# The r projection of an RWKV-7 layer, moved from the dense part into the pairs' projection jobs of the scan

## The chip, the core and the metric

The kernel runs on one core of a Trainium2 chip. The time is the device time of one execution in microseconds (us), from launch to end. The engines are TensorE (PE, whose weight loads are listed as PEld), VectorE (DVE), ScalarE (ACT), GpSimd (POOL) and SyncE (SP), which here only issues DMA transfers. Each engine works through its own queue in order and waits on semaphores for the others. TensorE's clock has two levels, 2.4 GHz and 1.2 GHz; the profile gives the granted share, 1.0 or 0.5, and its mean over a stretch.

## What is computed

One step of a two-layer network over 640 tokens (512 of a sample, 128 of a prompt) with 1024 features. Each layer is a SwiGLU feed-forward, a token mixer and a second feed-forward. Layer 0's mixer is a bidirectional RWKV-7, and only this is touched:

```python
xx = 0.5 * (hp[:, :-2] + hp[:, 2:]) - h
xs = h[None] + xx[None] * mu[:, None, None, :]
xr, xw, xk, xv, xa, xg = xs[0], xs[1], xs[2], xs[3], xs[4], xs[5]
rkv = jnp.einsum('nbtd,nde->nbte', jnp.stack([xr, xk, xv]), w_rkv)
...
def step(S, inp):
    r_t, w_t, k_t, v_t, kk_t, a_t = inp
    sa = jnp.einsum('bhij,bhj->bhi', S, -kk_t)
    S = (S * w_t[:, :, None, :]
         + sa[..., None] * (kk_t * a_t)[:, :, None, :]
         + v_t[..., None] * k_t[:, :, None, :])
    return S, jnp.einsum('bhij,bhj->bhi', S, r_t)
```

Six token streams are mixed from h and its neighbours. Three of them (r, k, v) go through 1024 x 1024 projections; the others through low-rank maps that give decays, rates and a gate. The recurrence then runs over the tokens in both directions, for 16 heads of 64.

## The kernel before

Features lie on the partitions, eight tiles of 128, and a tile of output features is a pair of heads, so there are eight pairs, 0 to 7. Tokens are cut into a first half of 384 and a second of 256 (in the dense part the cut is at 382, so that a token's neighbours are in the same part).

**The dense part** (`dense`) follows the first feed-forward. For each half and for each stream in `ORDER`, `stream` builds eight tiles on VectorE (line 466), stores them to DRAM if they are needed later (`keep`, line 470, streams 2 and 3 for k and v), and `project` multiplies them on TensorE in full float32 (line 502). Only pair 0's k and v are made here (`VD = 1`). Then come pair 0's key norm (lines 552 to 563), the gate's second map for all pairs (line 570) and, last, r for all eight pairs (lines 574 to 589): stream 0 is built and cut into a high and a low float32r part, each pair's weights as well (`wsplit`), and `mm3` makes three float32r products for one (lines 299 to 301), over 382 and 260 columns. The result goes through ACT (line 588) to DRAM, row `rkv[0][m]`.

**The scan** (`scan`) works on the pairs in overlapping periods. Pair m's `chain`, which carries the states from chunk to chunk, takes period m; its `products` and `solve` stand in period m - 1, its `prep` (loads of r, k, v, key transposes at line 744, decays) in period m - 2, and its `proj` (k and v, for pairs 1 to 7) in period m - 3. Each stage is a generator. `scan` gives each step a due time, spread evenly over the stage's window (`WIN`), and issues whichever is due first; the order in which instructions then stand on the engines is fixed when the program is built, by a scheduler that may move independent work a little. The periods have no fixed length: the chip runs the queues as they stand.

**A projection job** (`proj`) does its products in float32 over 320 columns: for j = 1, 2 (k, v) and each half of the tokens, eight products accumulate in bank `px`, with weights in `pw` tiles and the stream's tiles reloaded from DRAM into a ring of four (`mid`). A step ends after two products. The result is copied by ACT (`po`) and stored. Each such product shows as two records in the trace.

Other names: `c` products of the chain are lines 938, 949, 957 (bank `pc`), its outputs lines 975 to 981 (`po`), the products inside chunks line 810 (`pg`) and the transposed keys 819 (`pa`), the solve's recurrence lines 880 and 882 on VectorE, and its end, blocks of 32 x 32 products, lines 904, 905, 911 and 912 (`pm`). From the fifth period on, 60 products that nobody reads (`filler`, line 638) fill in for the projections.

Of the kernel before, what the change touches and what calls it, by code (L numbers as in the profile page):

```python
# [14 lines left out]
ALU = mybir.AluOpType  # L15
# [25 lines left out]
class Net:  # L41
# [15 lines left out]
    def psum(self, tag="ps"):  # L57
        """the next of a tag's banks"""
        if isinstance(tag, int):
            return self.ps.tile([P, 512], F32, tag=f"b{tag}", name=self.name("ps"))  # L60
        q = self.banks[tag]
        q.append(q.pop(0))
        return self.ps.tile([P, 512], F32, tag=f"b{q[-1]}", name=self.name(tag))
# [29 lines left out]
    def silu_cond(self):  # L93
        """2 silu(cond), on every partition"""
# [10 lines left out]
    def mods(self, layer, idx, ks=range(KD)):  # L105
        """modulation vector idx of a layer -> [P, KD, 2]"""
# [11 lines left out]
    def mods_first(self):  # L118
        """the first two modulation vectors, on the tensor engine"""
# [35 lines left out]
    def premod_scale(self, layer, sub, scale):  # L155
        """norm_pre * (1 + scale) -> [P, KD, 2]"""
# [13 lines left out]
    # -- 1/sqrt(mean + eps) of every token, from sums over each partition's features --  # L170
    def rstd(self, ss, n, eps, bank=None):
        """bank: a PSUM bank whose contents are no longer needed"""
# [28 lines left out]
    def part(self, hf, k, lo, dt=F32R):  # L201
        """one of the two parts of tile k of a product's moving operand"""
        return self.fp.tile([P, PARTW[hf]], dt, tag=f"h{'hl'[lo]}{hf}_{k}", name=self.name("hp"))

    def sumsq(self, srcs, hf):
        """sum over the tiles of squares, per partition"""
# [15 lines left out]
    def postnorm_gen(self, fps, hf, gp, eps, bank=None):  # L222
        """x += gp * f * rstd(f), f in PSUM; stops after the first half of the tiles"""
# [25 lines left out]
    def prenorm_gen(self, hf, gs, sh, dest, bank=None, r=None):  # L249
        """h = x * rstd(x) * gs + sh, every piece to the place that dest(tile, half) names"""  # L250
# [34 lines left out]
    def wsplit(self, src, eng=None):  # L285
        """a [P, up to 1024] block of weights as its two parts"""
# [16 lines left out]
    def ffn_s1(self, fi, hs, lead=0, early=()):  # L303
        """hs: per half a function that gives (hi, lo) tiles; returns g tiles"""
# [60 lines left out]
    def s2_step(self, hf, banks, outs, wh, wl, gh, gl, zero, first, last):  # L365
        """zero: zeros to open the banks with that two outputs share"""
# [15 lines left out]
ORDER = (1, 2, 4, 3, 5)  # L382
# [3 lines left out]
WQ = 256  # L386
FILL = (60, 4.8, 7.3)
# [3 lines left out]
class Rwkv:  # L391
# [31 lines left out]
    # Tokens 0..381 are one part of every stream, the rest the other: 382..511, two that mean nothing, the prompt.  # L423
    def dense_open(self, dram):
# [3 lines left out]
        self.xs = {j: dram.tile([P, KD, NT], F32, tag=f"xs{j}", name=f"xs{j}") for j in (1, 2)}  # L428
# [16 lines left out]
    def cut(self, hf, t, o=0):  # L445
        """the values of a part, o to the right"""
# [27 lines left out]
    def split_stream(self, i, hf):  # L474
        """a stream's part, every tile in two parts"""
        n, nc = self.n, self.nc
        out = []
        for k in range(KD):
            v, h, l = (self.view(hf, x) for x in (n.tmp(hf, WIDE[hf]), n.part(hf, k, 0), n.part(hf, k, 1)))
            nc.vector.scalar_tensor_tensor(v, self.xx[hf][k], self.vec[:, i, k:k + 1], self.cut(hf, self.h[hf][k], 1),  # L480
                                           op0=ALU.mult, op1=ALU.add)
            nc.scalar.activation(h, v, AF.Copy)
            (nc.vector if k % 3 == 1 else nc.gpsimd).tensor_tensor(l, v, h, op=ALU.subtract)  # L483
            out.append((h, l))
        return out

# [9 lines left out]
    def project(self, ws, xs, hf):  # L496
        """-> per block of weights [(first token, last, values in PSUM)]"""
# [11 lines left out]
    def dense(self, first):  # L509
        """first: the decay stream's part of the first tokens"""  # L510
# [29 lines left out]
        wr = {j: [self.load_w(t["w_rkv"][j, m]) for m in range(VD)] for j in (1, 2)}  # L540
        for hf in range(2):
            for i in ORDER:
                j = {2: 1, 3: 2}.get(i)
# [30 lines left out]
        xs = [self.split_stream(0, hf) for hf in range(2)]  # L574
        for m in range(KD):
            wh, wl = n.wsplit(t["w_rkv"][0, m])
            p = [self.view(hf, n.psum()) for hf in range(2)]
# [892 lines left out]
```

## Time and profile before

| | us |
|---|---|
| time, median of 3 runs | 3125.17 (3123.72 to 3130.29) |
| span of the profiled execution | 3110.3 |
| first feed-forward, up to the streams | about 0 to 541 |
| dense part without r | about 541 to 614 |
| r for all pairs | 614 to 677 |
| scan, periods -2 to 7 | 677 to about 1500 |
| rest of layer 0, and layer 1 | 1500 to 3110 |

The profiled execution's span runs from its first to its last instruction; it is a single execution, and its time stands beside the runs' as 3110.3 beside 3125.17. The periods' bounds are read from the times at which one pair's px products end and the next pair's begin: 677, 724, 780 (period 0), 884, 978, 1075, 1166, 1262 (period 5). In the tables of stretches, a busy time is the union of an engine's instructions; for TensorE it includes the last product's way through the array. The busy time of TensorE over the whole span is 2907.5 us (93%), of VectorE 1864.6 (60%), of ACT 1082.9 (35%) and of POOL 581.7 (19%).

### The profile page before, as it was taken

Reading aid. Unit: us, or ns where it says so; the run is one execution under the profiler, and the core shown is the slowest. Engines: PE = TensorE matmul, PEld = TensorE weight load, DVE = VectorE, ACT = ScalarE, POOL = GpSimd, SP = SyncE. Lnnn points to the kernel's source line nnn. Section 1 sums busy time; section 2 is a strip of 40 time slices with the busy share of each in tenths; the row PEclk is TensorE's granted clock in tenths of the full one; section 3 lists DMA queues with packets and bytes.
Section 4 is the critical chain, followed back from the end, with each engine's and each line's share of the span. In section 5 each row is a group of like instructions: output and inputs, shape, how many; then the busy total and the mean of one; then the engine's idle time right before and its main releaser. Section 6 shows DMA issues by size and latency. Waiting matters only on the chain.

```text
span 3110.3 us, 52692 instructions
## 1 busy us (share of the span) xinstructions
PE 2907.5 (93%) x21118; PEld 2588.4 (83%) x21118; DVE 1864.6 (60%) x3695; ACT 1082.9 (35%) x1892; POOL 581.7 (19%) x601
## 2 busy tenths in 40 slices
PE   8999998799999999999879999999999986999998
PEld 5999998585666666666779999999999986999997
DVE  7996338915647766566679995573333478432336
ACT  3122234423434444444341222452222455321233
POOL 2000033212212221121320002420001443000034
PEclk8999999997778888878889999999999997999999
DMA  6664235424323332012416664332212432222233
GB/s 242 215 215 165 89 122 187 152 97 148 96 79 106 120 104 90 30 48 78 165 56 208 224 224 160 128 106 95 82 68 102 140 120 85 82 75 76 89 122 123
DMA packets 163734, 382.05 MB, mean 123 GB/s; under 512 B 22432, under 2 KB 84512, under 8 KB 163232
## 3 DMA queue, kind: packets, MB, share of 16 engines
q1 hardware_dynamic: 161472, 375.60, 35.9%
q8 instruction: 166, 2.72, 0.4%
q10 hardware_dynamic: 2016, 3.07, 0.3%
q14 instruction: 80, 0.66, 0.1%
HBM read 352.19 MB, written 26.41 MB: 122 GB/s over the span
## 4 chain that ended last, share of the span: by engine, by line
PE 49%; DVE 7%; ACT 3%; issue 1%; DMA 0%; POOL 0%; SPq 0%; DVEq 0%; ACTq 0%; POOLq 0%
PE ps L300 14%; PE ps L299 14%; PE ps L301 14%; PE px L638 1%; DVE t L215 1%; DVE t L239 1%; ACT t L266 1%; PE pg L810 1%; DVE wl L294 1%; DVE t L242 0%; PE pa L737 0%; PE pc L949 0%; DVE x L243 0%; DVE sx L882 0%; ACT hp L275 0%
## 5 line engine op out<-in xcount | busy, mean ns | idle before, releaser
L299 PE MATMUL ps<-hp,wh 128*128 128x384 f32 (+2 forms) x3008 | 932.8, 312 | 14.7 <-ACT hp L275 10.4
L300 PE MATMUL ps<-hp,wh 128*128 128x384 f32 (+2 forms) x3008 | 934.4, 311 | 4.9 <-DVE hp L483 2.0
L301 PE MATMUL ps<-hp,wl 128*128 128x384 f32 (+2 forms) x3008 | 930.1, 310 | 2.9 <-DVE wl L294 2.9
L294 DVE TENSOR_TENSOR wl<-raw,wh 128x1024 fp32r<-128x1024 f32 x353 | 439.4, 1250 | 470.3 <-ACT wh L293 469.8
L293 ACT ACTIVATE wh<-raw 128x1024 fp32r<-128x1024 f32 x369 | 389.5, 1059 | 820.6 <-PE ps L300 693.5
L299 PEld LDWEIGHTS ps<-hp,wh 128*128 128x128 f32 x3008 | 569.8, 190 | 17.9 <-ACT hp L275 12.2
L300 PEld LDWEIGHTS ps<-hp,wh 128*128 128x128 f32 x3008 | 572.1, 190 | 6.9 <-DVE hp L483 2.2
L301 PEld LDWEIGHTS ps<-hp,wl 128*128 128x128 f32 x3008 | 569.3, 189 | 5.3 <-DVE wl L294 5.0
L350 POOL TENSOR_TENSOR gl<-t,gh 128x384 fp32r<-128x384 f32 (+1 forms) x176 | 237.7, 1352 | 1558.5 <-ACT gh L349 1528.2
L301 PE MATMUL ps<-gh,wl 128*128 128x384 f32 (+1 forms) x1408 | 438.0, 312 | 4.1 <-DVE wl L294 4.1
L300 PE MATMUL ps<-gl,wh 128*128 128x384 f32 (+1 forms) x1408 | 436.1, 310 | 3.1 <-POOL gl L350 3.1
L299 PE MATMUL ps<-gh,wh 128*128 128x384 f32 (+1 forms) x1408 | 435.7, 310 | 2.7 <-ACT gh L349 2.7
L113 DVE CUSTOM_DVE_ANT_0 cj<-raw,cj,bmod 128x1024 bf16<-128x1024 f32 x264 | 341.3, 1293 | 12.0 <-DMA raw<-in_w_mod 7.8
L301 PEld LDWEIGHTS ps<-gh,wl 128*128 128x128 f32 x1408 | 268.6, 191 | 5.2 <-DVE wl L294 4.3
L300 PEld LDWEIGHTS ps<-gl,wh 128*128 128x128 f32 x1408 | 267.8, 190 | 5.0 <-POOL gl L350 4.3
L299 PEld LDWEIGHTS ps<-gh,wh 128*128 128x128 f32 x1408 | 268.2, 191 | 4.4 <-ACT gh L349 3.3
L323 ACT ACTIVATE t<-ps 128x384 f32<-128x384 f32 (+1 forms) x176 | 75.6, 430 | 383.8 <-PE ps L301 383.8
L667 PE MATMUL px<-mid,pw 128*128 128x320 f32 x448 | 190.9, 544 | 3.4 <-DMA mid<-xs 2.0
L325 DVE TENSOR_TENSOR t<-t,ps 128x384 f32<-128x384 f32 (+1 forms) x176 | 85.4, 485 | 157.5 <-PE ps L301 157.0
L324 DVE SCALAR_TENSOR_TENSOR t<-t,ps 128x384 f32<-128x384 f32 (+1 forms) x176 | 85.0, 483 | 118.1 <-ACT t L323 118.0
L667 PEld LDWEIGHTS px<-mid,pw 128*128 128x128 f32 x448 | 88.3, 225 | 41.0 <-issue 18.4
L882 DVE TENSOR_TENSOR sx<-sx,spr 128x30 f32<-128x30 f32 (+14 forms) x240 | 100.5, 419 | 4.0
(393 smaller groups left out, 3600.7 us busy)
## 6 DMA issues: line engine op xcount, KB each, us to landing
raw<-in_w SPq DMA_DIRECT2D x352, 512.0 KB, 3.3
raw<-in_w_mod SPq DMA_DIRECT2D x132, 512.0 KB, 4.2
mid<-xs SPq DMA_DIRECT2D x224, 160.0 KB, 2.3
pw<-in_w_rkv SPq DMA_DIRECT2D x28, 256.0 KB, 3.1
raw<-in_w_o SPq DMA_DIRECT2D x9, 512.0 KB, 5.1
d<-po SPq DMA_DIRECT2D x28, 160.0 KB, 2.3
w<-in_w_mod_first SPq DMA_DIRECT2D x8, 512.0 KB, 7.8
raw<-in_w_rkv SPq DMA_DIRECT2D x8, 512.0 KB, 4.7
```

The costliest lines, as they stand in the source:

```text
L113: nc.vector.tensor_tensor_reduce(self.junk, w, self.cond[:, i], 0.5, self.bmod[:, layer, idx, k:k + 1], ALU.mult, ALU.add, out[:, k, i:i + 1])
L293: nc.scalar.activation(h, w, AF.Copy)
L294: (eng or nc.vector).tensor_tensor(l, w, h, op=ALU.subtract)
L299: nc.tensor.matmul(out, wh, xh, start=start, stop=False)
L300: nc.tensor.matmul(out, wh, xl, start=False, stop=False)
L301: nc.tensor.matmul(out, wl, xh, start=False, stop=stop)
L323: nc.scalar.activation(gt, o[0], AF.Tanh, scale=0.5)
L324: nc.vector.scalar_tensor_tensor(gt, gt, 1.0, o[0], op0=ALU.add, op1=ALU.mult)
L325: nc.vector.tensor_tensor(gt, gt, o[1], op=ALU.mult)
L350: nc.gpsimd.tensor_tensor(gl, g, gh, op=ALU.subtract)
L667: nc.tensor.matmul(p[:, 0:320], w[k // 4][:, k % 4 * P:k % 4 * P + P], x, start=k == 0, stop=k == KD - 1)
L882: nc.vector.tensor_tensor(X[:, i + 1:32, 0:i], X[:, i + 1:32, 0:i], pv, op=ALU.add)
```

## The change

`split_stream` and the r loop at the end of `dense` go. Stream 0 becomes the fifth of six in `ORDER`, is kept in DRAM like streams 2 and 3, and gives pair 0's r in full float32 through `project`. For pairs 1 to 7, `proj` runs over j = 0, 1, 2: r first, then k and v as before. The job now has 25 steps. Its window stays one period long; the first eight steps (r) are spread over the first 32% of it (`RW`), the other 17 over the rest. Doc strings and comments are dropped as well, so the line numbers of the changed kernel are lower by 23 in the scan.

```diff
-ORDER = (1, 2, 4, 3, 5)
+ORDER = (1, 2, 4, 3, 0, 5)
+RW = 0.32
...
-        self.xs = {j: dram.tile([P, KD, NT], F32, tag=f"xs{j}", name=f"xs{j}") for j in (1, 2)}
+        self.xs = {j: dram.tile([P, KD, NT], F32, tag=f"xs{j}", name=f"xs{j}") for j in (0, 1, 2)}
...
-        wr = {j: [self.load_w(t["w_rkv"][j, m]) for m in range(VD)] for j in (1, 2)}
+        wr = {j: [self.load_w(t["w_rkv"][j, m]) for m in range(VD)] for j in range(3)}
...
-                j = {2: 1, 3: 2}.get(i)
+                j = {0: 0, 2: 1, 3: 2}.get(i)
...
-        xs = [self.split_stream(0, hf) for hf in range(2)]
-        for m in range(KD):
-            wh, wl = n.wsplit(t["w_rkv"][0, m])
-            p = [self.view(hf, n.psum()) for hf in range(2)]
-            for k in range(KD):
-                q = slice(k * P, (k + 1) * P)
-                for hf in range(2):
-                    n.mm3(p[hf], wh[:, q], wl[:, q], *xs[hf][k], k == 0, k == KD - 1)
...
-            save(self.rkv[0][m], o)
...
-                elif name != "proj" or m >= VD:
+                elif name != "proj":
                     jobs.append([w0, rank, make(S[m]), (w1 - w0) / cnt])
+                elif m >= VD:
+                    jobs.append([w0, rank, make(S[m]), RW * (w1 - w0) / 8, 8, (1 - RW) * (w1 - w0) / cnt])
...
                 e[0] += e[3]
+                if len(e) > 4:
+                    e[4] -= 1
+                    if e[4] == 0:
+                        e[3] = e[5]
...
-        for j in (1, 2):
+        for j in range(3):
             w = [self.tile_("pw", [P, 512], 3) for _ in range(2)]
```

How the change moves instructions, at three places of TensorE's queue. A row is line, operation, out<-in with buffer numbers, and the size of the output; xN stands for N equal rows in a run.

First, the end of the dense part. Before, the last products of r stand ahead of the key transposes of pair 0 (L744), the first product of the scan:

```order
L299 MATMUL ps_6315<-hp_5855,wh_6310 128x260
L300 MATMUL ps_6315<-hp_5856,wh_6310 128x260
L301 MATMUL ps_6315<-hp_5855,wl_6311 128x260
L744 MATMUL pa_6407<-ident,ta_1039_6404 128x128 x3
L861 MATMUL pm_6791<-ident,v_6398 128x128 x4
L744 MATMUL pa_6416<-ident,ta_1039_6404 128x128 x2
L861 MATMUL pm_6808<-ident,v_6398 128x128
L667 MATMUL px_6391<-mid_5323,pw_6387 128x320 x4
```

In the changed kernel the gate's products (L558, line 570 before) stand there, and L721 is the key transpose, L644 the px product:

```order
L558 MATMUL ps_5842<-gm_5326,w_5768 128x384
L558 MATMUL ps_5845<-gm_5326,w_5768 128x256
L721 MATMUL pa_5889<-ident,ta_957_5882 128x128 x3
L721 MATMUL pa_5898<-ident,ta_957_5882 128x128 x2
L838 MATMUL pm_6326<-ident,v_5876 128x128 x4
L644 MATMUL px_5869<-mid_5324,pw_5865 128x320 x4
L714 MATMUL pa_5912<-mid_5324,lw_5880 128x384
```

No r product is left between the gate and the scan.

Second, the end of the solve in a period of the scan, TensorE again. Before, the first block of 32 x 32 products stands in the next pair's period, behind its first products inside chunks and transposed keys:

```order
L819 MATMUL pa_8951<-ident,bk_1368_8522 128x128 x4
L667 MATMUL px_8929<-mid_5323,pw_8925 128x320 x2
L1011 MATMUL po_8894<-blk_6381,psq_8891 128x2 x3
L1007 MATMUL po_9005<-pdc_8878,k_6377 128x256
L904 MATMUL pm_8696<-sb_8655,ga_8041 32x32
L905 MATMUL pm_8696<-sb_8655,a_1322_8269 32x32
```

In the changed kernel (L881 is line 904, L915 is 938, L958 is 981) the block of the same kind stands in the period before it, behind the first products of that pair's last chain step and a px product:

```order
L956 MATMUL po_9005<-gr_7652,uv_7897 64x64 x2
L958 MATMUL po_9005<-gr_7652,uv_7897 64x64 x2
L915 MATMUL pc_8561<-st_8556,ar_1175_7205 64x64 x2
L915 MATMUL pc_8561<-st_8556,ar_1205_7512 64x64 x2
L644 MATMUL px_9358<-mid_5324,pw_9182 128x320
L881 MATMUL pm_9275<-sb_9234,ga_8588 32x32
L882 MATMUL pm_9275<-sb_9234,a_1386_8817 32x32
```

The four blocks have moved ahead of the next pair's first chain step, and px products stand before and after the first two.

Third, the products inside the chunks early in a period. Before, with k's px products:

```order
L957 MATMUL pc_8907<-uv_8282,bt_8043 64x64 x4
L810 MATMUL pg_9017<-ar_1392_8803,bk_1393_8804 128x128
L819 MATMUL pa_9046<-ident,bk_1368_8522 128x128 x2
L819 MATMUL pa_9046<-ident,bk_1393_8804 128x128 x2
L667 MATMUL px_8929<-mid_5323,pw_8926 128x320
L957 MATMUL pc_8907<-uv_8282,bt_8043 64x64 x4
L667 MATMUL px_8929<-mid_5323,pw_8926 128x320
```

In the changed kernel (L787 is line 810, L934 is 957, L796 is 819), with r's:

```order
L787 MATMUL pg_9564<-ar_1431_9071,bk_1432_9072 128x128
L787 MATMUL pg_9565<-ar_1431_9071,bk_1432_9072 128x128
L644 MATMUL px_9520<-mid_5324,pw_9517 128x320 x2
L934 MATMUL pc_9498<-uv_8834,bt_8590 64x64 x4
L796 MATMUL pa_9594<-ident,bk_1432_9072 128x128 x4
```

The px products stand in groups of two instead of singly, between the same steps of the chain; from the start of a pair's chain to the next pair's key transposes there are 16 in place of some 13.

From the first filler products on, in period 5, the two queues are alike again apart from where the last of the blocks stand.

## Rows read from the trace of the kernel before

**Rows 1.** The page: span; the clock in 40 slices.

```profile
span 3110.3 us, 52692 instructions
PEclk8999999997778888878889999999999997999999
```

**Rows 2.** Windows: length, busy us (count) of PE, PEld, DVE, ACT, POOL; clock; DMA.

```profile
614.00:677.00 63.00, 59.52 (x389) 58.60 (x387) 11.49 (x20) 15.23 (x47) 10.58 (x8) 0.95 0.28 95
677.00:724.00 47.00, 39.25 (x153) 22.94 (x151) 18.66 (x38) 14.99 (x31) 16.76 (x21) 0.89 0.60 186
724.00:780.00 56.00, 51.88 (x258) 30.30 (x256) 28.99 (x77) 22.88 (x36) 8.92 (x10) 0.73 0.43 131
780.00:884.00 104.00, 96.54 (x827) 62.70 (x825) 65.31 (x157) 42.78 (x78) 25.76 (x30) 0.70 0.30 93
884.00:978.00 94.00, 85.93 (x862) 58.38 (x862) 60.88 (x155) 42.45 (x79) 22.34 (x29) 0.85 0.33 101
978.00:1075.00 97.00, 89.39 (x864) 62.44 (x862) 62.39 (x159) 43.19 (x80) 22.37 (x29) 0.81 0.33 99
1075.00:1166.00 91.00, 82.90 (x875) 57.22 (x871) 62.42 (x160) 43.23 (x81) 22.68 (x32) 0.89 0.34 107
1166.00:1262.00 96.00, 88.22 (x849) 59.78 (x848) 60.59 (x157) 43.09 (x80) 22.02 (x27) 0.80 0.28 86
```

**Rows 3.** TensorE timeline, both ends of the r stage: start us, us, what.

```profile
614.02 0.52 PE L299 MATMUL ps<-hp,wh 128*128 128x382 f32 x1
...
676.63 0.49 PE L744 MATMUL pa<-ident,ta 128*128 128x128 f32 x3
```

**Rows 4.** Windows inside two scan periods: early, late, early, late half.

```profile
987.00:1025.00 38.00, 37.02 (x339) 28.21 (x339) 10.58 (x41) 12.01 (x25) 2.34 (x5) 0.55 0.13 38
1033.00:1080.00 47.00, 41.20 (x445) 26.15 (x445) 44.26 (x103) 20.68 (x44) 20.11 (x24) 1.00 0.48 148
1087.00:1116.00 29.00, 28.04 (x301) 21.45 (x301) 9.88 (x39) 9.59 (x24) 2.35 (x5) 0.71 0.14 42
1124.00:1171.00 47.00, 42.39 (x446) 26.75 (x446) 43.60 (x102) 20.13 (x43) 20.10 (x24) 0.96 0.48 149
```

**Rows 5.** TensorE lines, 614 to 677 us: busy us, mean ns, idle before.

```profile
L300 PE MATMUL ps<-hp,wh 128*128 128x382 f32 (+1 forms) x128 | 40.6, 317 | 3.5 <-DVE hp L483 2.0 <-POOL hp L483 1.5
```

**Rows 6.** TensorE lines by form, dense part, 521 to 614 us.

```profile
L502 PE MATMUL ps<-t,w 128*128 128x382 f32 x64 | 24.5, 528 | 10.0 <-DVE t L466 10.0
L502 PE MATMUL ps<-t,w 128*128 128x260 f32 x80 | 19.1, 389 | 2.6 <-DVE t L466 2.3
```

**Rows 7.** px products: the page's group; TensorE timeline at full and half clock.

```profile
L667 PE MATMUL px<-mid,pw 128*128 128x320 f32 x448 | 190.9, 544 | 3.4 <-DMA mid<-xs 2.0
...
687.88 1.34 PE L667 MATMUL px<-mid,pw 128*128 128x320 f32 x4
689.15 0.70 PE L737 MATMUL pa<-mid,lw 64*128 64x256 f32 x2
...
1019.93 2.50 PE L667 MATMUL px<-mid,pw 128*128 128x320 f32 x4
```

**Rows 8.** Windows of line L667 alone, an early and a late half.

```profile
987.00:1025.00 38.00, 7.45 (x12) 3.02 (x12) 0.55 0.13 38
1033.00:1080.00 47.00, 14.21 (x40) 6.20 (x39) 1.00 0.48 148
```

**Rows 9.** TensorE timeline, a block of 32x32 products: first and last.

```profile
986.97 0.22 PE L904 MATMUL pm<-sb,ga 32*32 32x32 f32 x1
...
988.05 0.23 PE L905 MATMUL pm<-sb,a 32*32 32x32 f32 x1
```

**Rows 10.** Waits of SP's queue and of TensorE, 677 to 1262 us.

```profile
SPq L666 <- PE px L667: 305.7, 137, 13.6
...
PE px L667 <- DMA mid<-xs: 2.0, 3, 1.1
```

More of the change, by code (lines that the diff above doesn't have):

```diff
@@ L471, in stream @@
             out.append(v)
-        return out
-    def split_stream(self, i, hf):
-        n, nc = self.n, self.nc
-        out = []
-        for k in range(KD):
[L479 to L484, printed above, removed]
         return out
@@ L572, in dense @@
             save(self.gate[m], o)
-        xs = [self.split_stream(0, hf) for hf in range(2)]
-        for m in range(KD):
-            wh, wl = n.wsplit(t["w_rkv"][0, m])
-            p = [self.view(hf, n.psum()) for hf in range(2)]
-            for k in range(KD):
-                q = slice(k * P, (k + 1) * P)
-                for hf in range(2):
-                    n.mm3(p[hf], wh[:, q], wl[:, q], *xs[hf][k], k == 0, k == KD - 1)
-            o = two()
-            for hf in range(2):
-                for a, b, v in self.pieces(hf, p[hf]):
-                    for (c0, c1), e in zip(HALF, o):
-                        x0, x1 = max(a, c0), min(b, c1)
-                        if x0 < x1:
-                            nc.scalar.activation(e[:, x0 - c0:x1 - c0], v[:, x0 - a:x1 - a], AF.Copy)
-            save(self.rkv[0][m], o)
     def key_norm(self, m, sm, yi, a):
```

## The prediction

> **What bounds the kernel now.** I read first the page's span and clock line [rows 1], then the stretches by stage, then, inside one scan period, the two halves of it, and last single lines and the order. The kernel is a chain of stages and TensorE carries all of them; the change touches two, the tail of the dense part and the scan. In the tail, from 614.02 to 676.63 us, TensorE does nothing but the r projection of all eight pairs, at clock 0.95, and the other engines stand nearly still: VectorE is busy 11.49 of 63 us [rows 2]. The first product of the scan, the key transposes L744, stands behind it in TensorE's queue [rows 3]. So this stage is serial, and what leaves it comes off the end.
>
> In the scan TensorE is also the fullest engine: 82.90 of 91 us to 89.39 of 97 us in periods 1 to 4, VectorE about 62 [rows 2]. But a period has two halves [rows 4]. Early on (987 to 1025, 1087 to 1116) the products inside the chunks and the end of the solve run: TensorE 37.02 of 38 and 28.04 of 29 us, VectorE about 10, the clock at 0.55 and 0.71. Later (1033 to 1080, 1124 to 1171) the solve's recurrence and the next pair's rows run: VectorE 44.26 and 43.60 of 47 us, TensorE 41.20 and 42.39, the clock at 1.00 and 0.96. The period is a chain of a stretch that TensorE sets and one that VectorE sets.
>
> **What is removed: the r stage.** TensorE passes from L299 at 614.02 to L744 at 676.63, 62.6 us [rows 3]; its 384 products waited only 3.5 us [rows 5]. Its casts (ACT), subtractions (VectorE, GpSimd) and eight weight blocks lay beside them.
>
> **What is added in the dense part.** Pair 0's r, two more projections. One over 382 columns costs 24.5 us / 64 records x 16 = 6.1 us, one over 260 columns 19.1 / 80 x 16 = 3.8 us [rows 6]: 9.9 us. The streams' multiply-adds on VectorE are the same 16 as the r stage's, and VectorE loses eight weight splits. In this part TensorE waits 10.0 and 2.3 us for streams [rows 6], which could swallow all of it (0); if VectorE's 16 multiply-adds come onto the path as well, it is some 16 us. I take +8.5, near the full price, since the two halves are ordered by the same streams. The gate products stay. **Dense: -62.6 + 8.5 = -54 us, between -63 and -47.** The 24 stores of the r stream on SP replace 16 stores of r and 8 weight loads; they land while TensorE does the gate, and should they not, only the first px products wait.
>
> **What is added in the scan.** Per pair 16 px products, 112 in all. At full clock two of them, four records, take from 687.88 to 689.15 us, 0.635 us each; at half clock two show 2.50 us, 1.22 each without the tail [rows 7]. Per pair that is 10.2 us or 19.5. At the present mix (190.9 us for 224) it is 0.85 each, 95 us in all [rows 7]. Against this stand:
>
> Cover. TensorE's idle time is 7.6 to 8.1 us a period (97 less 89.39, 91 less 82.90), 7.7 in the first period (47 less 39.25), 4.1 in the second [rows 2]. These are waits for the chain's VectorE and ACT steps. The order shows the new products between just such steps; I take 5 us a period, 4 in the first, 2 in the second.
>
> Clock. Time at half clock in a period is 2 x (1 - clock) x length: 20 us in the 91 us period, 37 in the 97 us one, 62 in the 104 us one [rows 2]. From the first two, 17 us more at half clock made the period 6 us longer, 0.36 us for each; 0.5 would be the bound. The clock was 1.00 in a late half with 40 px records (20 products) in 47 us and 0.55 in an early half with 12 (6 products) in 38 us [rows 8]. At the head of that early half stand blocks of 40 products of 32x32, about 1.1 us each [rows 9], four to a period. By the order they now stand at the end of the period before, with px products between, and the stretch from the next pair's first chain step to its key transposes holds 16 px in place of some 13 with the blocks among them. With 48 px in some 92 us every part of a period gets about what the late half had. I take 11 us at half clock in place of 30 on average in periods 1 to 4 (20 to 38), 25 of 62 in period 0, 12 of 30 in the second period.
>
> Sum. First period (677 to 724): +10.2 - 4 = +6. Second (724 to 780): 10.2 + 0.6 for the clock - 2 - 0.43 x 18 = +1. Period 0: 10.8 - 5 - 0.4 x 37 = -9. Periods 1 to 4: 10.8 - 5 - 0.4 x 19 = -2 each, -8. From period 5 on the order is the same and fills with products of its own: 0. **Scan: -10 us, between -44 and +95.** The ends are full clock throughout, and no cover and no refund.
>
> **What costs nothing.** SP gets 20 more transfers a pair, past the loads of the next rows, the bonus and the gate; it already sits 305.7 us waiting for TensorE to free px tiles, and px waited 2.0 us for its own [rows 10]: bounds 0 and +1 per period, I take 0, since loads are issued at least a ring of four tiles ahead. If that cover went, each row load would add its landing to the solve's half. ACT gets two copies a pair, with ACT at 43 of 97 us [rows 2].
>
> **Total.** 3110.3 - 54 - 10 = 3046 us of span. The median of the runs, 3125.17, lies 14.9 above the span of the profiled execution; with the same between them the forecast is 3061.
>
> **The rivals.** (a) *No refund, slower.* The clock stays as it is and TensorE, the fullest engine, pays 95 us less at most 20 of cover: +75 - 54 = 3146, and 3166 without cover. It decides at 54 us, or 7.7 us a pair. For it speaks that plain TensorE work grows (71 us at full clock for 54 removed); against it, the clock of the halves. In the early half TensorE was busy 37.02 of 38 us and still got 0.55 [rows 4]. My chance for it is 0.10. The Trainium skill (TensorE: Matmul & The Clock Gate, "Why this matters for your kernels") lays the loss of the clock to idle gaps between bursts of products and keeps an engine without such gaps at full rate. By that rule more products give nothing back where TensorE is already busy, and the time is this rival's, 3146; the trace disagrees in the early half, busy 37.02 of 38 us at 0.55.
>
> (b) *A new wait.* The 32x32 blocks now stand in TensorE's queue ahead of the chain's last step and the next pair's first, and they wait for the solve on VectorE; with 13 more px in the half that VectorE sets (44.26 of 47) the half grows by the px' full 8 us in periods 0 to 5 and the refund is used up: 6 x 8 = +48 on a scan without gain, about 3119, no change. For it speaks how full both engines are there; against it, that the next chain cannot pass its second step before the solve anyway. 0.09.
>
> (c) *Full clock.* Periods 1 to 4 at 94.5 - 0.4 x 30 + 10.2 - 5 = 88, 7 less than now, period 0 at about 84, the first two together +4: scan -28 - 20 + 4 = -44, time 3027. 0.15.
>
> (d) *The scan's start is held by something else* than TensorE's queue (pair 0's key norm, its loads behind the gate's stores): 15 us of the 54 are lost, 3076. That r isn't moved at all is excluded by the order. 0.05.
>
> **How the numbers follow.** The forecast has 0.61, and its own range is 3038 to 3090. (c) lies below, (b) and (a) above. Leaving out the lower half of (c), the upper half of (b) and all of (a), some two in ten, the range is 3025 to 3113. A measurement of this kernel can tell about 0.2%, 6 us, from no change. Faster: forecast, (c), (d) and a third of (b), 0.84. Same: 0.05. Slower: (a) and the rest, 0.11.
>
> **What would show it.** The key transposes should start near 622 us in place of 676.63, with no products in between but the gate's; the px line should count 672 records; periods 1 to 4 should last 88 to 96 us at a clock of 0.90 or more, their early half above all; a block of 32x32 products should not have more than 2 us of wait before it. I am wrong if the clock of the early half stays under 0.75 (then (a)), or if the wait before the blocks is 5 us or more (then (b)), or if the key transposes start after 635 us.

## The result, and the profile after

The changed kernel takes 3074.68 us (median of 4 runs, 3070.31 to 3077.74) beside 3124.44 us of the kernel before in the same series; the ratio is 0.9859, with a 95% interval of 0.9825 to 0.9893. In a second series it took 3074.52 us beside 3116.7 (ratio 0.9863, 0.9838 to 0.9888). So it is faster by 1.4%, about 43 us of 3117 (the medians lie 49.8 and 42.2 us apart). The forecast, 3061, was 14 us too low; its range, 3025 to 3113, holds the time.

The page of the changed kernel, its span and the clock in 40 slices, to lay beside [rows 1]:

```profile
span 3076.0 us, 52654 instructions
PEclk8999999999898889878889999999999997999999
```

The four 7s in a row in [rows 1] (slices 10 to 13), the first periods of the scan, are gone; the single 7 further on is still there.

The r stage first. The ends of the dense part in TensorE's timeline (start us, us, what), first stream product and first key transpose:

```profile
544.40 1.45 PE L490 MATMUL ps<-hp,w 128*128 128x382 f32 x4
...
631.07 0.49 PE L721 MATMUL pa<-ident,ta 128*128 128x128 f32 x3
```

That is 86.7 us. In the kernel before the first stream product started at 540.66 us and the key transposes at 676.63 [rows 3], 136.0 us apart. The dense part is 49.3 us shorter. (The 3.7 us by which it starts later lie in code that was not touched; the first stream product started between 540.7 and 545.6 us in the profiles of this study, whatever the kernel.)

The windows of the scan of the changed kernel (as in [rows 2]: length, busy us of PE, PEld, DVE, ACT, POOL, clock, DMA), from the key transposes, with bounds where a pair's last chain output stands:

```profile
631.07:680.00 48.93, 40.92 (x166) 23.41 (x165) 18.10 (x38) 16.47 (x31) 17.07 (x22) 0.93 0.72 219
680.00:742.00 62.00, 53.52 (x297) 32.17 (x296) 32.85 (x81) 23.21 (x38) 8.14 (x9) 0.94 0.61 185
...
798.00:899.50 101.50, 97.01 (x956) 65.54 (x957) 66.28 (x183) 49.40 (x94) 22.16 (x30) 0.94 0.49 145
899.50:996.70 97.20, 90.58 (x900) 60.11 (x900) 59.77 (x160) 44.31 (x83) 21.08 (x29) 0.88 0.45 135
996.70:1093.90 97.20, 90.83 (x899) 60.28 (x898) 59.49 (x160) 44.44 (x83) 22.96 (x29) 0.88 0.45 135
1093.90:1191.20 97.30, 90.76 (x900) 60.06 (x899) 59.55 (x160) 44.36 (x83) 21.09 (x29) 0.88 0.45 134
```

The second stretch runs at 0.94 in place of 0.73, so the clock did come up. But the steady periods take 97.2 us each, about as long as the 91 to 97 us before, with the clock at 0.88 and 6.4 to 6.6 us of idle time in each. Inside them, an early and a late half (to lay beside [rows 4]):

```profile
1044.00:1081.00 37.00, 34.40 (x329) 24.01 (x330) 16.79 (x57) 16.14 (x30) 3.29 (x8) 0.92 0.34 102
1081.00:1128.00 47.00, 44.82 (x403) 28.17 (x400) 39.71 (x99) 19.42 (x40) 15.34 (x18) 0.91 0.55 167
```

The early half has risen from 0.55 and 0.71 to 0.92. Part of this is the order: the blocks of 32x32 products, with which the first window of [rows 4] begins, now lie ahead of the early half. Counted from the first block on, it is at 0.82 and 0.85 in two periods:

```profile
935.80:984.00 48.20, 45.59 (x487) 31.52 (x487) 16.43 (x53) 21.78 (x40) 5.53 (x11) 0.82 0.35 106
1032.40:1081.00 48.60, 46.00 (x496) 31.78 (x498) 17.61 (x59) 23.08 (x42) 5.75 (x12) 0.85 0.35 106
```

The whole scan, from the key transposes to the chain's last output, of the kernel before and of the changed one:

```profile
676.63:1500.24 823.61, 759.27 (x7095) 509.16 (x7093) 488.73 (x1260) 353.30 (x668) 183.00 (x237) 0.82 0.30 92
```

```profile
631.07:1466.33 835.26, 773.74 (x7317) 512.76 (x7316) 480.17 (x1260) 361.45 (x682) 179.04 (x238) 0.88 0.40 121
```

The scan has become 11.7 us longer in these two executions. Idle time of TensorE (length less busy) went from 64.3 to 61.5 us; time at half clock (2 x (1 - clock) x length) from about 296 to 200.

### The profile page after: what moved, and what is told of

The parts are those of the page before. It is cut to its first block, busy times and chain, and to the rows that moved or that the text cites. A ratio compares the mean times of both kernels' runs of the same rounds, so it can differ in the third digit from the quotient of the medians.

```text
span 3076.0 us, 52654 instructions
## 1 busy us (share of the span) xinstructions
PE 2876.2 (94%) x20990; PEld 2542.1 (83%) x20990; DVE 1840.9 (60%) x3681; ACT 1071.6 (35%) x1853; POOL 562.9 (18%) x591
## 4 chain that ended last, share of the span: by engine, by line
PE 71%; DVE 15%; ACT 5%; issue 4%; DMA 3%; POOL 1%; SPq 0%; DVEq 0%; ACTq 0%; POOLq 0%
PE ps L300 17%; PE ps L299 17%; PE ps L301 17%; PE px L644 5%; DVE cj L113 2%; PE pg L787 2%; DVE t L215 1%; DVE sx L859 1%; PE px L615 1%; PE ps L490 1%; ACT sab L810 1%; ACT t L266 1%; PE pa L714 1%; DVE wl L294 1%; PE pc L926 1%
## 5 line engine op out<-in xcount | busy, mean ns | idle before, releaser
L299 PE MATMUL ps<-hp,wh 128*128 128x256 f32 (+1 forms) x2880 | 892.5, 312 | 16.7 <-ACT hp L275 10.4
L300 PE MATMUL ps<-hp,wh 128*128 128x256 f32 (+1 forms) x2880 | 894.4, 311 | 2.0 <-POOL hp L1305 0.8
L301 PE MATMUL ps<-hp,wl 128*128 128x256 f32 (+1 forms) x2880 | 889.8, 310 | 3.1 <-DVE wl L294 3.1
L294 DVE TENSOR_TENSOR wl<-raw,wh 128x1024 fp32r<-128x1024 f32 x345 | 426.7, 1240 | 461.8 <-ACT wh L293 461.6
L293 ACT ACTIVATE wh<-raw 128x1024 fp32r<-128x1024 f32 x361 | 381.2, 1059 | 827.8 <-PE ps L300 692.4
L299 PEld LDWEIGHTS ps<-hp,wh 128*128 128x128 f32 x2880 | 545.1, 190 | 19.9 <-ACT hp L275 12.2
L300 PEld LDWEIGHTS ps<-hp,wh 128*128 128x128 f32 x2880 | 547.2, 190 | 3.5 <-POOL hp L1305 1.1
L301 PEld LDWEIGHTS ps<-hp,wl 128*128 128x128 f32 x2880 | 544.3, 189 | 5.4 <-DVE wl L294 4.9
L644 PE MATMUL px<-mid,pw 128*128 128x320 f32 x672 | 251.1, 501 | 12.1 <-DMA mid<-xs 7.1
L644 PEld LDWEIGHTS px<-mid,pw 128*128 128x128 f32 x672 | 127.0, 211 | 73.1 <-issue 22.6
L859 DVE TENSOR_TENSOR sx<-sx,spr 128x30 f32<-128x30 f32 (+14 forms) x240 | 109.9, 458 | 3.9
```

What stands on the lines that cost most here:

```text
L293: nc.scalar.activation(h, w, AF.Copy)
L294: (eng or nc.vector).tensor_tensor(l, w, h, op=ALU.subtract)
L299: nc.tensor.matmul(out, wh, xh, start=start, stop=False)
L300: nc.tensor.matmul(out, wh, xl, start=False, stop=False)
L301: nc.tensor.matmul(out, wl, xh, start=False, stop=stop)
L644: nc.tensor.matmul(p[:, 0:320], w[k // 4][:, k % 4 * P:k % 4 * P + P], x, start=k == 0, stop=k == KD - 1)
```

## The experiments

Each series ran on one chip beside its own runs of the kernel before. "Idle" and "at half" are read from the row of the scan of each profile, as above; a clock of two digits leaves some 8 us of doubt in the last column.

| run | median, us (runs) | before beside it | ratio, 95% interval | scan | idle | at half |
|---|---|---|---|---|---|---|
| kernel before (first profile) | | | | 823.6 | 64.3 | 296 |
| changed (first series) | 3074.68 (4) | 3124.44 | 0.9859, 0.9825 to 0.9893 | 835.3 | 61.5 | 200 |
| e1_no_r_scan | 3075.94 (4) | 3113.2 | 0.9872, 0.9849 to 0.9895 | 829.8 | 65.8 | 315 |
| e2_r_half | 3067.32 (4) | 3113.2 | 0.9849, 0.9827 to 0.9872 | 824.9 | 61.2 | 247 |
| e3_stores_act | 3075.45 (4) | 3113.2 | 0.9876, 0.9854 to 0.9898 | 834.7 | 61.4 | 184 |
| e4_shift_late | 3084.26 (6) | 3113.2 | 0.9904, 0.9883 to 0.9926 | 832.8 | 71.2 | 150 |
| e5_after_again | 3074.52 (6) | 3116.7 | 0.9863, 0.9838 to 0.9888 | 835.2 | 60.9 | 184 |
| e6_no_r_again | 3062.41 (6) | 3116.7 | 0.9842, 0.9814 to 0.987 | 837.1 | 65.3 | 318 |
| e7_r_twice | 3127.99 (12) | 3116.7 | 1.0037, 1.0022 to 1.0053 | 883.1 | 50.4 | 194 |
| e8_fill90 | 3090.0 (6) | 3116.7 | 0.9914, 0.9892 to 0.9936 | 849.1 | 60.3 | 170 |
| e9_fill30 | 3074.04 (6) | 3115.83 | 0.9862, 0.9832 to 0.9892 | 841.0 | 68.6 | 252 |
| e10_rw16 | 3087.82 (11) | 3115.83 | 0.9916, 0.9888 to 0.9944 | 868.6 | 68.7 | 243 |
| e11_no_r_at_all | 3051.08 (6) | 3116.36 | 0.979, 0.9759 to 0.9821 | 825.9 | 65.1 | 297 |
| e12_r_last | 3059.19 (6) | 3116.36 | 0.9815, 0.9788 to 0.9841 | 818.1 | 53.4 | 147 |

### What the dense part gave and what pair 0's r costs: e11 and e3

The changed kernel without any r, which reads k in place of it for all pairs:

```diff
-ORDER = (1, 2, 4, 3, 0, 5)
+ORDER = (1, 2, 4, 3, 5)
...
-        wr = {j: [self.load_w(t["w_rkv"][j, m]) for m in range(VD)] for j in range(3)}
+        wr = {j: [self.load_w(t["w_rkv"][j, m]) for m in range(VD)] for j in (1, 2)}
...
-        for j in range(3):
+        for j in (1, 2):
...
-        for o, j in ((k, 1), (r, 0), (v, 2)):
+        for o, j in ((k, 1), (r, 1), (v, 2)):
```

> The changed kernel with no r anywhere: neither pair 0's r (stream 0 is not built, stored or multiplied) nor that of pairs 1 to 7 (all pairs read k in place of r, so the outputs are not the network's). From the first stream product to the first key transpose the kernel before took 136.0 us, the changed one 86.7, without r in the scan 85.6 and 85.2. Theory 1 (the old r stage was serial, 62.6 us, and pair 0's r costs 12 to 13 us in the dense part): 73.4 us there (72 to 75). Rival (part of the old stage lay beside other work, and pair 0's r costs the 8.5 us forecast or less): 77 us or more. The total should lie some 12 us under that of the kernel without r in the scan: 3052 to 3060.

Its TensorE timeline has the first stream product and the first key transpose 71.0 us apart:

```profile
542.67 1.45 PE L490 MATMUL ps<-hp,w 128*128 128x382 f32 x4
...
613.64 0.49 PE L721 MATMUL pa<-ident,ta 128*128 128x128 f32 x3
```

From 136.0 that is 65.0 us less: the old r stage was serial in full, with 2.4 us on top of its 62.6. Pair 0's r then costs 86.7 less 71.0, 15.7 us (14.2 and 14.6 in e6 and e1, where the dense part took 85.2 and 85.6), even more than Theory 1 expected. The total fell to 3051.08 us, just below the 3052 to 3060 expected.

Part of the 15.7 us shows on SyncE's queue in the second half of the dense part of the changed kernel (start us, us the queue was taken, what), and in VectorE's waits there:

```profile
592.80 7.44 SPq L471 DMA_DIRECT2D xs<-t  x16
600.33 0.86 SPq L525 DMA_DIRECT2D d<-ev  x2
601.28 7.79 SPq L471 DMA_DIRECT2D xs<-t  x16
609.16 0.86 SPq L525 DMA_DIRECT2D d<-ev  x2
610.11 7.78 SPq L471 DMA_DIRECT2D xs<-t  x16
```

```profile
DVE t L467 <- DMA xs<-t: 6.2, 10, 1.4
```

A tile of a stream has two stores in this half, and SyncE needs 0.49 us to issue each (7.79 / 16): 16 stores take 7.8 us, where VectorE makes the eight tiles in 3.9 (8 x 484 ns). Three streams are now stored there, in a row without a pause, so VectorE waits 6.2 us for tiles to come free; before it was 1.3. Run e3 issues the r stream's stores from ScalarE:

```diff
-                    nc.sync.dma_start(self.xs[keep][:, k, a:b], q)
+                    (nc.sync if keep else nc.scalar).dma_start(self.xs[keep][:, k, a:b], q)
```

> The changed kernel with the 24 stores of the r stream issued by ScalarE in place of SyncE. Theory 1 (in the second half of the dense part SyncE's issues, 48 stores of about 0.49 us each without a pause from 592.80 to 618.89 us, pace the streams, and VectorE waits 6.2 us for them to free its tiles): the key transposes start 5 to 8 us earlier after the first stream product, total 3067 to 3070. Rival (the 16 multiply-adds on VectorE, 0.48 and 0.61 us each, or the 9.9 us of products set it): less than 2 us.

```profile
DVE t L467 <- DMA xs<-t: 3.2, 7, 0.7
```

The wait halved and the dense part of its profile took 83.2 us, 3.5 less than 86.7: SyncE's issues are a part of the price, though less than Theory 1 asked for. How the rest divides between the products (9.9 us by the prediction's estimate) and VectorE's multiply-adds no run shows. The total, 3075.45, shows no gain: 3.5 us is less than one execution of the scan differs from the next.

### What r costs in the scan: e1, e6, e2, e5, e7

Run e1, and e6 once more beside the changed kernel (e5): r of pairs 1 to 7 left out of the scan, whose TensorE order is then that of the kernel before.

```diff
-                    jobs.append([w0, rank, make(S[m]), RW * (w1 - w0) / 8, 8, (1 - RW) * (w1 - w0) / cnt])
+                    jobs.append([w0, rank, make(S[m]), (w1 - w0) / cnt])
...
-        for j in range(3):
+        for j in (1, 2):
...
-        for o, j in ((k, 1), (r, 0), (v, 2)):
+        for o, j in ((k, 1), (r, 0 if m < VD else 1), (v, 2)):
```

> The changed kernel with the 112 r products of pairs 1 to 7 left out of the scan (their pairs read k in place of r, so those outputs are not the network's). TensorE's order in the scan is then that of the kernel before. Theory 1 (r's products cost their full-clock price, about 0.63 us each, hardly any of it in TensorE's idle time, and give back half of every microsecond that the clock is no longer low): from the first key transpose to the chain's last output 823 us, as before, in place of 835; idle time of TensorE about 64 us as before, time at half clock back from 193 to about 290 us; total 3063. Rival (r's products lie in idle time and the 12 us come from the moved 32x32 blocks): idle time goes up by some 30 us or more, total also near 3063; the two are told apart by the idle time, and by the half dose. Second rival (the 12 us are the spread of single executions): 3073 to 3077.

> The changed kernel itself, beside the kernel without r in the scan on the same chip, since single executions of one kernel lie up to 8 us apart and what r costs in the scan is of that size. Theory 1 in its first size (the scan is 12 us longer with r, as the two profiles say): 3076 where the kernel without r is at 3064. Theory 1 with a larger refund (the clock gives back nearly all of the 71 us): the two within 4 us.

> The changed kernel without the r products of pairs 1 to 7 in the scan once more, beside the changed kernel (the outputs are then not the network's). See there: 12 us faster than it by the first size, within 4 us by the second.

The scan rows of e1 and e6:

```profile
628.50:1458.30 829.80, 764.02 (x7093) 513.60 (x7093) 490.53 (x1260) 354.91 (x670) 184.00 (x239) 0.81 0.31 92
```

```profile
629.20:1466.30 837.10, 771.84 (x7094) 516.91 (x7093) 489.26 (x1260) 355.34 (x670) 184.29 (x239) 0.81 0.31 91
```

The same order took 823.6 (before), 829.8, 837.1 and 825.9 us (e11) in four profiles, 829.1 on average; idle time stood within 1.5 us, and the longest scan had the most time at half clock. With r it took 835.3 and 835.2: +6, not +12. In time, e5 lies 12 us above e6 by medians and 8 by means; e6's runs fell into two groups (3058.8 to 3063.5, and 3076.4 and 3079.0), and e1 on another chip lay at 3075.94. So r's price in the scan as the change places it is some 6 us, between 0 and 12, and these runs do not settle it closer. What they do settle is how it is made up: idle time fell by 4 us only (65.1 on average to 61.2), while time at half clock fell by some 107 to 123. The rival as it was priced, 30 us or more of idle time, is out; in small a part of it is there, as the waits by line show further down.

Half the dose, four feature tiles of r in place of eight, at the same due times and with the blocks where the change put them:

```diff
-                for k in range(KD):
+                for k in range(KD if j else 4):
...
-                    if k % 2:
+                    if k % 2 or j == 0:
```

> The changed kernel with only four of the eight feature tiles of r in the scan: 56 r products in place of 112, at the same due times, with the 32x32 blocks where the change put them (the r of pairs 1 to 7 is then only a part of r). Theory 1: the work falls by 56 x 0.635 = 36 us, the idle time stays within 5 us of 61, time at half clock rises by about half of the 100 us that the change took away, so the scan comes to 829 (823 to 832). Rival (order): the scan stays at 835 or rises, since the moved blocks and not the products cost the 12 us; idle time rises by the 36 us of work that has gone, less what the clock takes.

```profile
628.40:1453.30 824.90, 763.68 (x7204) 506.07 (x7204) 480.98 (x1260) 359.35 (x680) 179.52 (x238) 0.85 0.37 111
```

824.9 us, below the scans with r in full where the change puts it and below the average without. 56 products are 36 us of work; the half clock went from some 307 us (average of the four) to 247, worth 30 at 0.5, and idle time gave 4. As far as one profile can tell, the first half of r is free in the scan; in time e2's median lies below e1's in the same series (3067.32 and 3075.94; e6, in another, had 3062.41). The moved blocks alone cannot be the price, since they are here too. Then the double dose:

```diff
-                    nc.tensor.matmul(p[:, 0:320], w[k // 4][:, k % 4 * P:k % 4 * P + P], x, start=k == 0, stop=k == KD - 1)
+                    z = 2 if j == 0 else 1
+                    for i in range(z):
+                        nc.tensor.matmul(p[:, 0:320], w[k // 4][:, k % 4 * P:k % 4 * P + P], x, start=k == 0 and i == 0, stop=k == KD - 1 and i == z - 1)
```

> The changed kernel with each of the 112 r products of the scan made twice (the sum halved afterwards): 224 in place of 112. Theory 1: 112 more at 0.635 us are 71 us of work; time at half clock had gone from 307 us (no r) over 242 (half) to 195 (all), so it can fall by some 50 to 80 us more, which gives back 20 to 35: net +35 to +50. Rival (idle time covers products): TensorE still has 61 us of idle time in the scan, so +10 or less. Second rival (no refund left): +71.

```profile
630.10:1513.20 883.10, 832.68 (x7540) 553.55 (x7540) 465.43 (x1260) 359.52 (x680) 195.17 (x238) 0.89 0.38 114
```

+48 us in the scan, at the upper end of Theory 1's range, and +53 in time over e5, just past it. The clock gave nothing more (194 us at half against 184 and 200); idle time gave 11, and TensorE's busy time rose by 58 us where 71 were estimated. So the refund runs out: large for the first 56 products, smaller for the next 56, none for the 112 beyond.

### Where in the job r stands: e10, e4, e12

Run e10 packs r's eight steps into the first 16% of the period:

```diff
-RW = 0.32
+RW = 0.16
```

> The changed kernel with r's eight steps in the first 16% of a projection job's period instead of 32%. The same products; r's stand closer together, and by the order the last three of four 32x32 blocks stand behind the first chain step of the next pair again, where the kernel before had them. Theory 1 (the price of r is its work less what the clock gives back; the blocks' place is no cost): idle time within 5 us of 61, total 3068 to 3080, and half clock less if the denser r lies behind the blocks. Rival (the moved blocks cost the scan time, as new waits): 8 us or more faster than the changed kernel.

Neither theory held. The time rose by 13 us and spread over 38 (3076.82 to 3114.65); the profile is of one of the longer executions (3108.97), its scan at a clock of 0.86 with 243 us at half, and its idle time rose by 7. A wait of the chain's products for VectorE (line 926, 742 to 1260 us) grew from 1.8 to 12.7 us in all. The blocks stand mostly where the kernel before had them, and nothing was won by it.

Run e4 moves every projection job later by 0.12 of a period:

```diff
-WIN = ((0, 0.8), (0, 0.95), (0, 0.3), (0.25, 1), (0.3, 1), (0, 1), (0, 1))
+WIN = ((0, 0.8), (0, 0.95), (0, 0.3), (0.25, 1), (0.3, 1), (0, 1), (0.12, 1.12))
```

> The changed kernel with every projection job moved by 0.12 of a period, so that projection products stand between the four 32x32 blocks at the end of the solve instead of a gap of some 11 us without any. Theory 1 (the clock falls just behind these blocks because too little dense work stands with them: 936.2, 1031.8, 1130.7 and 1229.7 us, each within 1.5 us of the first block): time at half clock in periods 1 to 4 falls from 24 us to 10 to 14 each, periods from 97 to some 92, total 3050 to 3062. Rival (the blocks bring the clock down whatever stands between them): time at half clock within 4 us of 24 per period, total 3070 to 3080. Second rival (a new wait, r's rows or k's late for the next stage): TensorE's idle time per period rises by 3 us or more, total over 3080.

(Of the four falls named there the last is 2.7 us behind its first block.) In the changed kernel the jobs of two pairs are some 11 us apart (px ends at 941.5 and starts again at 952.8 us), just where the blocks stand. With the job moved, px products stand between the blocks, and the window of the four blocks there (944.3 to 953.2 us in its profile) runs at full clock:

```profile
944.30:953.20 8.90, 8.90 (x190) 6.64 (x188) 2.25 (x11) 4.93 (x10) 2.27 (x2) 1.00 0.46 143
```

So in this profile the clock is higher, as Theory 1 expected (about 150 us at half in the scan), and the rival of blocks that slow it whatever stands between is out. Theory 1's reason, too little dense work with the blocks, is not borne out by the same profile. One period earlier px products stand between the blocks too, but the first block waited 3.69 us; from 846.1 to 863.2 us the clock was at half. The first block's row, and the stretches behind it and behind the block at 944.3:

```profile
845.01 0.22 PE L881 MATMUL pm<-sb,ga 32*32 32x32 f32 x1 [3.69 <-DVE kya L575]
845.00:862.00 17.00, 16.98 (x235) 11.90 (x236) 1.90 (x10) 8.58 (x15) 2.92 (x5) 0.53 0.26 72
944.30:961.00 16.70, 16.70 (x258) 11.95 (x256) 3.52 (x14) 6.66 (x14) 3.69 (x7) 1.00 0.52 151
```

The time did not follow: idle time rose by 10 us, with new waits of up to 1.6 us before px beside this one, and the kernel took 3084.26, as the second rival had it. The profile is of the fastest of the six executions (3075.19) with a mean clock of 0.952 over its span; the other five had 0.942 to 0.945, no more than the changed kernel's 0.943 to 0.949, so the gain in clock is shown for this execution only.

Run e12 has the same 25 even steps with k and v first and r last:

```diff
-                    jobs.append([w0, rank, make(S[m]), RW * (w1 - w0) / 8, 8, (1 - RW) * (w1 - w0) / cnt])
+                    jobs.append([w0, rank, make(S[m]), (w1 - w0) / 25])
...
-        for j in range(3):
+        for j in (1, 2, 0):
```

> The changed kernel with r as the last third of each projection job instead of the first, at even distances (25 steps over the period). The same products, the same density, another third of the period. Theory 1 (only the number of products and their even spread count, by way of the clock): total within 5 us of the changed kernel's 3074, idle time within 5 us of 61. Rival (it is the place early in the period that pays): 8 us or more slower.

```profile
632.40:1450.50 818.10, 764.75 (x7316) 508.99 (x7316) 472.01 (x1260) 359.99 (x682) 181.78 (x238) 0.91 0.42 123
```

Both theories fell, in the other direction: 3059.19, 15 us below the changed kernel, with all six runs (3052.63 to 3065.18) below all of e5's. The two stood in different series; by each one's ratio to the kernel before (0.9815 and 0.9863) it is still some 15 us. The mean clock was 0.952 to 0.956 in all six, beside e5's 0.943 to 0.949. It beats both kernels, and its scan is shorter than any without r. (With the r stream's stores on ScalarE as well it was not tried.) Its steady periods, beside the 97.2 us at 0.88 above:

```profile
893.30:982.50 89.20, 84.72 (x900) 57.25 (x900) 57.96 (x158) 44.12 (x83) 22.46 (x29) 0.98 0.50 147
982.50:1074.70 92.20, 87.92 (x900) 58.96 (x898) 58.36 (x161) 44.05 (x83) 22.45 (x29) 0.94 0.49 142
1074.70:1168.00 93.30, 88.41 (x899) 59.57 (x899) 58.74 (x161) 44.83 (x84) 22.86 (x30) 0.94 0.48 141
```

The place of the difference can be seen. TensorE's timeline and windows of the changed kernel around a first block (a bracket is idle time and what ended it):

```profile
932.87 0.45 PE L915 MATMUL pc<-st,ar 64*64 64x64 f32 x8 [0.69 <-DVE st L938]
933.24 0.81 PE L644 MATMUL px<-mid,pw 128*128 128x320 f32 x2
935.83 0.22 PE L881 MATMUL pm<-sb,ga 32*32 32x32 f32 x1 [1.78 <-DVE sb L868]
```

```profile
925.80:935.80 10.00, 7.56 (x85) 4.74 (x83) 9.93 (x14) 4.38 (x7) 4.68 (x4) 1.00 0.64 191
935.80:952.80 17.00, 16.98 (x221) 11.42 (x221) 1.85 (x4) 7.84 (x14) 3.61 (x7) 0.51 0.29 92
```

And the same with r last:

```profile
935.39 0.28 PE L954 MATMUL po<-ar,st 64*64 64x64 f32 x2
935.60 0.22 PE L881 MATMUL pm<-sb,ga 32*32 32x32 f32 x1
```

```profile
925.60:935.60 10.00, 10.00 (x109) 6.46 (x108) 9.83 (x20) 6.69 (x10) 4.47 (x6) 1.00 0.45 129
935.60:947.00 11.40, 11.40 (x230) 8.97 (x229) 1.84 (x2) 7.74 (x15) 3.76 (x6) 1.00 0.55 166
```

In the changed kernel TensorE runs dry just ahead of the block, idle for 2.4 of 10 us while VectorE, busy 9.93 of 10, ends the solve. Then the clock stands at half for nearly all of the 17 us until the next job's px products come, at 952.8. With r last nothing waits there, the next job's px products come 11.4 us behind the first block, and the clock stays at 1.00. (In both, px products also stand ahead of the second block; the stretch without any is 11.3 us in the one and 5.0 in the other.) The wait repeats: it stands ahead of the first block in periods 1 to 4 of the changed kernel, 1.4 to 1.8 us each, and once, 0.6 us, earlier; with r last there is none. The changed kernel's row of it (742 to 1235 us; us in all, times, longest):

```profile
PE pm L881 <- DVE sb L868: 7.0, 5, 1.8
```

The wait and the low clock go together. In the 14 profiles of this study 25 first blocks had 1.2 us or more of wait just ahead, and the clock fell within 3 us of the start of each; of the 64 that had less than 0.1 us, with the clock still full, it did so at one. But no run takes away the wait alone, and the clock also falls without it: in the kernel before at 990.6 us, some 4 us behind a first block with no such wait, and e10 has no wait just ahead of a first block yet 243 us at half clock with the same products. So the wait is not shown to be the cause, and it is not the only one.

### The products that nobody reads: e8, e9

```diff
-FILL = (60, 4.8, 7.3)
+FILL = (90, 4.8, 7.3)
```

> The changed kernel with 90 products that nobody reads in place of 60 in periods 5 to 7. In the changed kernel 52 of 91 us of one of these periods ran at half clock, in which no projection is left. Theory 1 (products without use raise the clock where it is low; the first ones pay, 65 us less at half clock for 36 us of work in the half dose of r): 30 x 0.61 = 18 us of work, 30 to 45 us less at half clock: between -4 and +4 in total. Rival (no refund): +18.

With 30 in place of 60:

```diff
-FILL = (60, 4.8, 7.3)
+FILL = (30, 4.8, 7.3)
```

> The changed kernel with 30 products that nobody reads in place of 60 in periods 5 to 7. With 90 the scan was 14 us longer at 22 us less of half clock. Theory 1 (each filler costs 0.6 us of work, and what the clock gives for it grows the fewer there are, as with r's half dose): work 18 us less, half clock 40 us or more longer, total within 5 us of the changed kernel's 3074. Rival (fillers buy nothing in the changed kernel, since the pairs' chain and not TensorE's clock sets these periods): 10 to 18 us faster.

90 cost 15.5 us of time (3090.0 against 3074.52): the clock gave little, 14 to 30 us less at half, and the rival's +18 is nearer than Theory 1's -4 to +4. 30 cost nothing (3074.04), as Theory 1 had it: half clock and idle time rose, by some 60 and 7 us, where 18 us of work went (its profile is of the longest of the six executions). It is the same curve as for r: from 30 to 60 the clock pays for the products, from 60 to 90 it hardly does.

## Why the prediction was right, and where it was not

**Against the profiled executions.** The forecast was a span of 3046; it became 3076.0. The 30 us are 3.7 in untouched code ahead of the dense part, 4.7 in the dense part (-49.3 for -54) and 21.7 in the scan (+11.7 for -10); the rest of the layers was the same within 0.4.

**The 14.9 us between span and median.** This was not a part of every execution. Span and time of one and the same execution differ by some 2 us (3076.0 and 3077.74; 3080.0 and 3082.11). The profiled execution of the kernel before was among its faster ones; its runs went from 3102.07 to 3130.84 over all series. Some 5 us of this lie in its scan, 823.6 beside an average of 829.1. So the two profiles show a scan that became longer by 12 where the averages say 6. The time missed by only 14 us where the span missed by 30 because these 14.9 us were added: that is luck.

**The removal, -62.6.** Right: e11 gives -65.0.

**Pair 0's r in the dense part, +8.5.** Too low: 14 to 16, the upper bound of the range that was given. The named cover failed: TensorE's waits for streams, 10.0 and 2.3 us, were still 10.0 and 3.5. And the stores of the r stream do not merely land while TensorE does the gate: 16 of them stand in a row of 48 that SyncE issues, and they hold VectorE's tiles (3.5 us by e3). The size is that of the case "if VectorE's 16 multiply-adds come onto the path as well"; that it was they is not shown.

**Cover in the scan, -31 in all.** This is the step that failed most. Idle time fell by 3 to 4 us. TensorE's waits in the scan show how (us in all, times, longest), of the kernel before and of the changed one:

```profile
PE pc L938 <- DVE st L961: 9.9, 8, 1.6
PE pc L957 <- ACT uv L951: 9.1, 13, 1.8
PE pc L949 <- DVE bs L944: 6.5, 8, 1.2
PE pa L744 <- ACT bt L820: 11.3, 6, 2.3
PE pm L904 <- DVE sb L891: 3.0, 3, 1.3
```

```profile
PE pc L915 <- DVE st L938: 6.3, 9, 1.5
PE pc L934 <- ACT uv L928: 2.1, 6, 0.7
PE pc L926 <- DVE bs L921: 1.8, 2, 1.0
PE pa L721 <- ACT bt L797: 16.4, 7, 3.0
PE px L644 <- DMA mid<-xs: 7.1, 15, 0.8
PE pm L881 <- DVE sb L868: 7.0, 5, 1.8
```

The cover came where the prediction saw it, at the chain's steps: the waits of its products (`pc`) fell from 25.5 to 10.2 us (9.9 in e5; 23.0 to 25.4 in the three profiles without r in the scan). But nearly as much came up in other places: 5.1 us before the key transposes, 4.0 before the 32x32 blocks, 5.1 before the px products for the stream's tiles (2.0 in [rows 10]), which the prediction took at 0. So the step counted the waits that the products would fill and not those that the new order and the added loads would make.

**The clock, -53.** Right in size: some 107 to 123 us less at half clock, worth 54 to 61 at 0.5, and e2 supports that price better than the 0.4 that was used. Wrong in place: the first two stretches got more (0.93, 0.94), the steady periods less (97.2 us at 0.88 where 88 to 96 at 0.90 or more were forecast): each kept some 23 us at half clock where 11 were forecast, 14 to 17 of them around the blocks. By doses the refund is not a rate: it is large at first and ends.

**The rivals.** (a) is out for this dose: the early half went to 0.92, and to 0.82 and 0.85 with the blocks, past the 0.75 at which it would have held. It describes the double dose (e7: +53 us for an estimated 71 us of work). (b), the wait at the 32x32 blocks, was seen and small in itself, 7.0 us in five places and at most 1.8 each; beside it stands the lost clock. By the rule of the Trainium skill (TensorE: Matmul & The Clock Gate, "Why this matters for your kernels"), which lays the loss to idle gaps between products, such a wait would have been the place to look. The trace agrees in kind, 2.4 idle us of 10 and then 0.51, though the page has longer gaps in mind than the single one of 1.78 us here; it disagrees in the early half of [rows 4], busy 37.02 of 38 us at 0.55. (c) did not come: even in e12, the best place found for the same products, the scan is 5.5 us shorter than before (818.1) where (c) asked for 44, and the total of 3059.19 is that of the forecast, 3061. (d) is out: the key transposes started at 631.07, before the 635 that was set, and px 7.1 us later where it had been 6.0.

So the mechanism, a serial stage taken out and a price in the scan mostly refunded by the clock, was right; cover and pair 0's price were too good, and the total came as near as it did by the 14.9 us that were added to the span.

## What to carry to other kernels

Work moved onto a full engine that spends much of its time at half clock can cost less than its price; count the refund from the time at half clock that is left, and expect the first part of the dose to get most of it. Do not count idle waits as cover without the waits that the new order makes: here some 15 us of them closed and 14 opened. When the same products can go first, spread or last in a job, try the places: here first and last differ by 15 us with the same work. And know how far single executions of the kernel lie apart before a term of 10 us is read from one profile each.

## What the hardware showed beyond what was expected

One kernel's executions on a single core lay up to 28 us apart (3102.07 to 3130.06 in one series of the kernel before), while the untouched part behind the scan took 1608.6 to 1614.2 us in all profiles. The longer executions had the lower clock (3102.07 us at a mean of 0.933, 3130.06 at 0.922), so much of the spread goes with the clock. Products that stood closer together (e10) did not get a higher clock: 0.933 to 0.950 over its runs, beside e5's 0.943 to 0.949, and the time spread over 38 us. The issue of a store on SyncE's queue took 0.49 us, so that tiles cut into two stores were made faster by VectorE (0.48 us) than they could be sent away.
